# When the products with the first two tiles' gathered rows may be placed on VectorE

## The chip, the cores and the metric

The kernel runs on one core of one Trainium2 chip. The metric is the device time of one launch in microseconds (us), compared over several runs of the kernel before and after. TensorE is called PE in the profile, VectorE DVE, ScalarE ACT, GpSimd POOL and SyncE SP.

## What is computed

One block of a diffusion model over 1024 latent tokens of width 1024, with 256 context tokens beside them. First a token-mixing part: an input projection, multi-head attention (8 heads, 1280 keys, low-rank queries), a state-space branch, gates, an output projection and a layer norm. Then a channel-mixing part, PEER: each token's queries pick 128 of 16384 experts (8 heads, 16 each), and the output is a weighted sum of their rows of `v`, with a weight from the dot product of the token with their rows of `u`:

```
experts = jnp.take_along_axis(cand_e, top_pos, axis=-1)
g = jax.nn.softmax(top_s, axis=-1).astype(xb.dtype)
act = jax.nn.gelu(jnp.einsum('thkd,td->thk', u_tab[experts], xb))
return jnp.einsum('thk,thkd->td', g * act, v_tab[experts])
```

After it comes a last layer norm, and the latent stream is the output.

## The kernel before, in words

The 1024 tokens are eight tiles of 128, numbered 0 to 7. They go through the front (attention, gates, output projection, first norm) in four groups: tile 0; tiles 1 and 2; tiles 3, 4 and 5; tiles 6 and 7 (`GROUPS`). For each group `front` runs these stages one behind another:

- `attention`: for each head and tile, scores on PE (L858 to L862), maximum on DVE (L863 to L867), exponential on ACT (L872), transposes and the product with the values (L805, L809). Keys and values come from DRAM by SP's queue.
- `gates`: projections (L239 to L241) with weights that SP loads and that ACT and DVE split in two parts (L233, L234).
- `close`: the output projection (L954 to L957), two layer norms (`affine`, L181 and L182, with a chain of small steps L142 to L154 for the reciprocal root), transposes (L192). At its end `prepare` (L770 to L780) makes the compressed queries of the next group; its last VectorE step for each tile is L775, and the last of these for group g is kept as the mark `p` with that group's index (the groups are counted from 0, so that `p2` is the third group's, of tiles 3 to 5, and `p3` the fourth group's, of tiles 6 and 7).
- `route`: it picks the experts. It is a generator, whose steps run beside the next group's attention; its last step (L1103) writes the experts' numbers of tiles that are not dense.

Tiles 2 to 5 (`DENSE`) are later multiplied with all experts in a PE-bound stage, `dense` (L1196 to L1198, L1235 to L1237), which takes the rest of the span; `spread` (L1147 to L1156) makes its table of weights during the fronts. Tiles 0, 1, 6 and 7 gather only the rows that they chose. The change concerns tiles 0 and 1. For each of them `score` makes 128 gathers, one row per token and choice (L1271: POOL issues an indirect DMA of 128 rows of 4 KB, 512 KB in all), and 128 products on DVE (L1275: row times token, summed into one number). `weighted` then gathers 128 times from `v` (L1351) and sums them on PE (L1356). Gathered rows of both kinds go through six buffers in turn (`RB = 6`), and each gather waits until the one six before it has been used. `retrieve` takes tile 0's products first, then 32 of tile 0's value rows, then tile 1's products with one value row of tile 0 after every second, then the values of tile 1.

The order of instructions on each engine is fixed when the program is built, by a scheduler that takes, among instructions that its model thinks ready, the one of highest priority. The fronts have a raised priority (`PRIO`), and the retrieval of tiles 0 and 1, traced behind all four fronts, has the lowest: its products fill what is left. Each engine then works through its own queue in that fixed order on the chip.

`HOLDS` adds an edge to that. For a tile in the table, each product from a given number on may be ordered on DVE only behind a marked DVE instruction:

```
held = [m for m, n in HOLDS[l] if s >= n] if l in HOLDS else []
with tc.issue_after(marks[held[-1]].ins) if held else nullcontext():
    V.scalar_tensor_tensor(ub, ub, 1.0, h2, op0=MUL, op1=MUL, accum_out=dots[:, s:s + 1])
```

With `S0 = 36`, `P0 = 128`, `M0 = "p2"` and `S1 = 100`, `P1 = 128`, `M1 = "p3"`, tile 0's products 36 to 127 stand behind `p2`, and tile 1's products 100 to 127 behind `p3`. The further entries of the two lists begin at products 164 (36 + 128) and 228 (100 + 128) and up, which a tile of 128 products does not have.

Of the kernel before, what the change touches and what calls it, by code (L numbers as in the profile page):

```python
# [73 lines left out]
S0 = 36  # L74
P0 = 128
S1 = 100
P1 = 128
M0 = "p2"
M1 = "p3"
HOLDS = {0: [(M0, S0)] + [("r1.%d" % h, S0 + P0 * (h + 1)) for h in range(8)],  # L80
         1: [(M1, S1)] + [("r2.%d" % h, S1 + P1 * (h + 1)) for h in range(8)],
         6: [("t3", 0)]}
KENG = ((), (), (), ())
GENG = ((), (), (), ())
EVERY = (1, 2, 1)
# [4 lines left out]
def block_kernel(ctx: ExitStack, tc: tile.TileContext, a: dict, out: bass.AP):  # L90
# [1173 lines left out]
    def score(l, ei, dots):  # L1264
# [4 lines left out]
        for s in range(128):  # L1269
            ub = rows.tile([128, D], F32, tag="row", name="ub")  # L1270
            GP.indirect_dma_start(out=ub, out_offset=None, in_=a["peer_u"],  # L1271
                                  in_offset=bass.IndirectOffsetOnAxis(ap=ei[:, s:s + 1], axis=0))
            held = [m for m, n in HOLDS[l] if s >= n] if l in HOLDS else []
            with tc.issue_after(marks[held[-1]].ins) if held else nullcontext():
# [320 lines left out]
```

## Time and profile before

| | us |
|---|---|
| runs of the kernel before: median (lowest to highest of 3) | 3748.12 (3733.66 to 3753.72) |
| the profiled execution, its own time | 3734.93 |
| span of the profiled execution | 3733.2 |
| PE busy in the span | 3359.1 (90%) |
| DVE busy in the span | 2956.9 (79%) |
| POOL busy in the span | 1491.9 (40%) |

The profile cuts the span into stretches and gives for each the busy time of each engine. Beside it stand the TensorE clock that was granted, as a share of full speed, the mean busy share of the core's 16 DMA engines, and what they moved. A count behind a busy time is a number of instructions. In a timeline, a bracket at the end of a line says how long the engine was idle before the instruction and what ended that. The profiled execution runs through the stages at these times: second group's attention from 653 to 849, its gates to 918, its close with `prepare` of the third group to 980, third group's attention from 994 to 1340, its gates from 1360 to 1520, its close with `prepare` of the fourth group to 1604, fourth group's attention from 1640 on, the dense stage from 2218 to the end.

### The profile page before, as it was taken

How to read it: one execution, taken by the hardware profiler on the slowest of the kernel's cores; microseconds unless marked ns; L12 is line 12 of the kernel's file. 1: busy time of each engine (PE TensorE's matmuls, PEld its weight loads, DVE VectorE, ACT ScalarE, POOL GpSimd, SP SyncE). 2: the span in 40 equal slices, each digit the busy share in tenths (PEclk: the TensorE clock that was granted, in tenths of full speed). 3: DMA queues.
4: the chain of work that ended last, by engine and by line, in shares of the span. 5: the costliest groups of instructions: out<-in, count | busy, mean ns of one | idle time of the engine just before them, and what ended most of it. 6: DMA issues, size and time to landing. Idle time of an engine off the chain costs nothing.

```text
span 3733.2 us, 54383 instructions
## 1 busy us (share of the span) xinstructions
PE 3359.1 (90%) x20022; PEld 2733.2 (73%) x20022; DVE 2956.9 (79%) x6996; ACT 1297.7 (35%) x2329; POOL 1491.9 (40%) x1254
## 2 busy tenths in 40 slices
PE   5978888979779989869999969999999999999997
PEld 3745577869667668757769758878888888888885
DVE  7358755685798879689968877888888888889895
ACT  2223353443123444033345443333333333333332
POOL 5045400041355564443442100265655555546540
PEclk7978999989889989979999979999999999999998
DMA  8742276476698898987898763599999999989992
GB/s 280 236 85 73 89 264 228 156 301 244 224 347 309 316 338 324 362 308 289 295 355 314 296 232 124 181 368 340 330 342 333 339 335 340 340 325 355 340 328 79
DMA packets 348714, 1032.46 MB, mean 277 GB/s; under 512 B 46592, under 2 KB 142080, under 8 KB 322592
## 3 DMA queue, kind: packets, MB, share of 16 engines
q0 software_dynamic: 147456, 536.94, 39.3%
q1 hardware_dynamic: 164032, 462.20, 34.9%
q10 hardware_dynamic: 36960, 29.86, 2.5%
q8 instruction: 157, 2.57, 0.3%
q14 instruction: 109, 0.89, 0.1%
HBM read 961.27 MB, written 67.62 MB: 276 GB/s over the span
## 4 chain that ended last, share of the span: by engine, by line
PE 56%; DVE 9%; issue 8%; DMA 7%; ACT 2%; POOL 2%; DVEq 0%; POOLq 0%; ACTq 0%
PE turn L1235 6%; PE turn L1237 6%; PE turn L1236 6%; PE fd L1196 5%; PE fd L1197 5%; PE fd L1198 5%; DMA vb<-in_peer_v,eiT 4%; DVE ub L1275 3%; PE po L954 2%; PE acc L1356 2%; PE pqr L1066 2%; PE pe L1153 2%; DMA ub<-in_peer_u,ei 2%; POOL ub L1271 1%; PE po L809 1%
## 5 line engine op out<-in xcount | busy, mean ns | idle before, releaser
L1271 POOL DMA_INDIRECT ub<-in_peer_u,ei x512 | 654.9, 1279 | 1212.9 <-DVE ub L1275 438.4
L1275 DVE SCALAR_TENSOR_TENSOR ub<-ub,h 128x1024 f32<-128x1024 f32 x512 | 616.3, 1217 | 59.5 <-DMA ub<-in_peer_u,ei 59.2
L1318 POOL DMA_INDIRECT vb<-in_peer_v,ei x256 | 361.8, 1413 | 268.2 <-DVE f L1321 205.5
L1351 POOL DMA_INDIRECT vb<-in_peer_v,eiT x256 | 288.7, 1128 | 400.4 <-PE acc L1356 324.8
L1235 PE MATMUL turn<-hh,u 128*128 128x512 f32 x1024 | 401.7, 392 | 0.0
L1236 PE MATMUL turn<-hh,u 128*128 128x512 f32 x1024 | 400.2, 391 | 0.0
L1237 PE MATMUL turn<-hl,u 128*128 128x512 f32 x1024 | 400.1, 391 | 0.0
L1197 PE MATMUL fd<-v,kpe_l 128*128 128x512 f32 x887 | 351.7, 397 | 1.5 <-DVE kpe_l L234 1.5
L1198 PE MATMUL fd<-v,kpe_h 128*128 128x512 f32 x887 | 349.6, 394 | 0.0
L1196 PE MATMUL fd<-v,kpe_h 128*128 128x512 f32 x887 | 339.3, 396 | 0.0
L1321 DVE SCALAR_TENSOR_TENSOR f<-vb,zz,f 128x1024 f32<-128x1024 f32 x254 | 325.4, 1281 | 2.8 <-DMA vb<-in_peer_v,ei 0.2
L1239 ACT ACTIVATE act<-turn 128x512 f32<-128x512 f32 x128 | 76.6, 598 | 578.7 <-PE turn L1237 578.6
L233 ACT CAST v<-w 128x1024 fp32r<-128x1024 f32 x128 | 134.7, 1053 | 269.1 <-PE fd L1197 269.0
L1235 PEld LDWEIGHTS turn<-hh,u 128*128 128x128 f32 x1024 | 192.3, 188 | 42.0
L1237 PEld LDWEIGHTS turn<-hl,u 128*128 128x128 f32 x1024 | 192.3, 188 | 41.9
L1236 PEld LDWEIGHTS turn<-hh,u 128*128 128x128 f32 x1024 | 192.3, 188 | 40.4
L1356 PE MATMUL acc<-vb,diag 128*32 128x256 f32 x2048 | 159.8, 397 | 51.1 <-DMA vb<-in_peer_v,eiT 51.0
L1198 PEld LDWEIGHTS fd<-v,kpe_h 128*128 128x128 f32 x887 | 166.8, 188 | 41.4
L1196 PEld LDWEIGHTS fd<-v,kpe_h 128*128 128x128 f32 x887 | 166.9, 188 | 40.8
L1197 PEld LDWEIGHTS fd<-v,kpe_l 128*128 128x128 f32 x887 | 166.9, 188 | 40.5 <-DVE kpe_l L234 1.8
L234 DVE TENSOR_TENSOR v<-w,v 128x1024 fp32r<-128x1024 f32 x128 | 156.2, 1221 | 33.4 <-ACT v L233 32.8
L1241 DVE TENSOR_TENSOR act<-act,gt 128x512 f32<-128x512 f32 x128 | 88.6, 692 | 118.2 <-ACT act L1239 117.9
(421 smaller groups left out, 8143.2 us busy)
## 6 DMA issues: line engine op xcount, KB each, us to landing
w<-in_peer_uT SPq DMA_DIRECT2D x64, 1024.0 KB
w<-in_peer_v SPq DMA_DIRECT2D x64, 1024.0 KB
w<-in_peer_wq SPq DMA_DIRECT2D x32, 1024.0 KB
gT_d<-stage SPq DMA_DIRECT2D x16, 2048.0 KB
gt<-gT_d SPq DMA_DIRECT2D x32, 1024.0 KB
vh<-v_d SPq DMA_DIRECT2D x32, 640.0 KB
w<-k_d SPq DMA_DIRECT2D x32, 640.0 KB
w<-in_w_mod_b SPq DMA_DIRECT2D x16, 1024.0 KB
```

What stands on the lines that cost most here:

```text
L1196: PE.matmul(o, ah[:, ts], vh[:, cs], start=first, stop=False)
L1197: PE.matmul(o, al[:, ts], vh[:, cs], start=False, stop=False)
L1198: return PE.matmul(o, ah[:, ts], vl[:, cs], start=False, stop=final)
L1235: PE.matmul(turn, uh[:, k, :], hh[:, k, :], start=(k == 0), stop=False)
L1236: PE.matmul(turn, ul[:, k, :], hh[:, k, :], start=False, stop=False)
L1237: PE.matmul(turn, uh[:, k, :], hl[:, k, :], start=False, stop=(k == 7))
L1271: GP.indirect_dma_start(out=ub, out_offset=None, in_=a["peer_u"], in_offset=bass.IndirectOffsetOnAxis(ap=ei[:, s:s + 1], axis=0))
L1275: V.scalar_tensor_tensor(ub, ub, 1.0, h2, op0=MUL, op1=MUL, accum_out=dots[:, s:s + 1])
L1318: GP.indirect_dma_start(out=vb, out_offset=None, in_=a["peer_v"], in_offset=bass.IndirectOffsetOnAxis(ap=ei[:, s:s + 1], axis=0))
L1321: V.scalar_tensor_tensor(f, vb, z[:, s:s + 1], f, op0=MUL, op1=ADD)
L1351: GP.indirect_dma_start(out=vb, out_offset=None, in_=a["peer_v"], in_offset=bass.IndirectOffsetOnAxis(ap=eiT[:, t:t + 1], axis=0))
L1356: PE.matmul(acc[d // 2][o:o + 32, 256 * (d % 2):256 * (d % 2) + 256], dg[:, q, jj, :], vb[:, d * 256:(d + 1) * 256], start=False, stop=Fal ...
```

## The change

The entries of tiles 0 and 1 leave the table of holds; that of tile 6 stays. The constants that they used stay unused, and no instruction is added or removed.

```diff
@@ -77,9 +77,7 @@
 P1 = 128
 M0 = "p2"
 M1 = "p3"
-HOLDS = {0: [(M0, S0)] + [("r1.%d" % h, S0 + P0 * (h + 1)) for h in range(8)],
-         1: [(M1, S1)] + [("r2.%d" % h, S1 + P1 * (h + 1)) for h in range(8)],
-         6: [("t3", 0)]}
+HOLDS = {6: [("t3", 0)]}
 KENG = ((), (), (), ())
 GENG = ((), (), (), ())
 EVERY = (1, 2, 1)
```

## Rows read from the trace of the kernel before

**Rows 1.** The page: the group of products (busy, mean ns, idle before).

```profile
L1275 DVE SCALAR_TENSOR_TENSOR ub<-ub,h 128x1024 f32<-128x1024 f32 x512 | 616.3, 1217 | 59.5 <-DMA ub<-in_peer_u,ei 59.2
```

**Rows 2.** Busy time by stretch: all engines, granted clock, DMA share, GB/s.

```profile
653.00:773.00 120.00, 112.24 (x800) 102.10 (x798) 85.20 (x375) 53.52 (x158) 4.89 (x6) 1.00 0.45 150
773.00:850.00 77.00, 56.02 (x337) 49.19 (x335) 64.95 (x130) 35.57 (x79) 47.94 (x35) 0.84 0.93 351
861.00:918.00 57.00, 54.46 (x455) 54.26 (x454) 30.58 (x39) 21.27 (x22) 0.00 (x0) 1.00 0.60 214
918.00:948.00 30.00, 30.00 (x138) 26.17 (x137) 14.95 (x40) 0.60 (x1) 0.00 (x0) 0.94 0.65 217
948.00:980.00 32.00, 23.19 (x169) 21.70 (x168) 21.52 (x87) 4.46 (x14) 0.00 (x0) 0.85 0.30 109
994.00:1160.00 166.00, 130.15 (x879) 114.14 (x877) 158.96 (x498) 51.24 (x133) 95.00 (x84) 0.90 0.94 346
1160.00:1232.00 72.00, 67.12 (x568) 48.72 (x569) 61.46 (x320) 21.03 (x57) 25.88 (x27) 0.95 0.74 262
1360.00:1520.00 160.00, 146.40 (x1228) 134.89 (x1228) 128.59 (x266) 59.75 (x67) 74.20 (x56) 0.96 0.90 337
1520.00:1581.00 61.00, 53.69 (x283) 41.47 (x284) 44.21 (x110) 1.79 (x3) 32.39 (x27) 0.94 0.93 350
1581.00:1604.00 23.00, 16.75 (x139) 13.93 (x137) 22.30 (x90) 3.38 (x7) 3.62 (x4) 0.87 0.74 288
1604.00:1640.00 36.00, 17.59 (x80) 9.76 (x81) 26.66 (x45) 9.31 (x19) 24.81 (x21) 0.56 0.90 318
1640.00:2217.00 577.00, 518.27 (x4148) 419.64 (x4148) 474.30 (x1706) 251.13 (x424) 181.33 (x174) 0.95 0.82 303
2217.00:3733.00 1516.00, 1484.38 (x6696) 1210.56 (x6695) 1287.57 (x2058) 494.74 (x690) 714.21 (x512) 0.99 0.83 298
```

The columns of this view are: stretch, length, PE, PE weight loads, DVE, ACT, POOL, then clock, DMA share and GB/s.

**Rows 3.** The same view for L1275 alone (two instructions a product, busy on DVE).

```profile
773.00:850.00 77.00, 40.78 (x68) 0.84 0.93 351
994.00:1160.00 166.00, 102.04 (x168) 0.90 0.94 346
1360.00:1520.00 160.00, 44.05 (x73) 0.96 0.90 337
1520.00:1581.00 61.00, 21.47 (x36) 0.94 0.93 350
```

**Rows 4.** Timeline of POOL, where the first hold ends.

```profile
981.64 1.68 POOL L1271 DMA_INDIRECT ub<-in_peer_u,ei  x1 [124.44 <-DVE ub L1275]
```

**Rows 5.** Timeline of DVE around the two marks (the accumulator reads are each product's second instruction).

```profile
979.61 0.62 DVE L775 TENSOR_SCALAR nq<-pa,rs_y 128x384 f32<-128x384 f32 x1
980.15 1.22 DVE L1275 SCALAR_TENSOR_TENSOR ub<-ub,h 128x1024 f32<-128x1024 f32 x1
...
1578.88 1.21 DVE L1275 SCALAR_TENSOR_TENSOR ub<-ub,h 128x1024 f32<-128x1024 f32 x1
...
1603.25 0.61 DVE L775 TENSOR_SCALAR nq<-pa,rs_y 128x384 f32<-128x384 f32 x1
1603.78 1.22 DVE L1275 SCALAR_TENSOR_TENSOR ub<-ub,h 128x1024 f32<-128x1024 f32 x1
...
1609.59 0.14 DVE L153 TENSOR_SCALAR rs_t<-rs_t 128x1 f32<-128x1 f32 x1
```

**Rows 6.** Timeline of PE behind the second mark.

```profile
1612.59 1.08 PE L1356 MATMUL acc<-vb,diag 128*32 128x256 f32 x8 [8.76 <-DMA vb<-in_peer_v,eiT]
1619.42 1.08 PE L1356 MATMUL acc<-vb,diag 128*32 128x256 f32 x8 [5.75 <-DMA vb<-in_peer_v,eiT]
...
1624.86 0.90 PE L778 MATMUL ptc<-eye,nq 128*128 128x128 f32 x3
```

**Rows 7.** Timeline of DVE: tile 1's experts are known.

```profile
1232.22 0.22 DVE L1103 CAST ei<-ef 128x128 int32<-128x128 f32 x1
```

**Rows 8.** Timeline of PE: the first product of the dense stage.

```profile
2217.65 0.48 PE L1235 MATMUL turn<-hh,u 128*128 128x512 f32 x1
```

## The prediction

> **What bounds the kernel now.** I read the table by stretch first, then the same table for the products alone, then the timelines at the two marks. The dense stage fills 2217 to 3733 with PE busy for 1484 of 1516 us [rows 2], and its first product runs at 2217.65 [rows 8]. Nothing of the change lies in it, so the change is worth what it moves this start. Before that the four fronts run one behind another, and the time of each stage is set by PE's work and by what delays PE. As a yardstick I take PE's busy time times the granted clock as its work, and the rest of a stretch as lost. The last attention stretch before any product, 653 to 773, loses 120 - 112.24 x 1.00 = 7.8 us, 6.5%. With products it is another stage: 773 to 850 loses 77 - 56.02 x 0.84 = 29.9 us, and 994 to 1160 loses 166 - 130.15 x 0.90 = 48.9 us, with DVE busy for 158.96 of 166 [rows 2]. The granted clock shows part of it: 1.00 before the first product, 0.84 and 0.90 beside them.
>
> The first hold is easy to see. POOL's gather at 981.64 had idled for 124.44 us behind a product that waited [rows 4], and that product runs at 980.15, right behind `p2` at 979.61 [rows 5]. Meanwhile DVE was busy for 30.58 of 57, 14.95 of 30 and 21.52 of 32 us [rows 2], so 52 us of it lay idle in the gates, the output projection and `prepare`. The second hold lasts from the product at 1578.88 to the one at 1603.78 [rows 5], but there DVE was full: 22.30 of 23 us [rows 2].
>
> **The change, part by part.** Nothing is added or removed. 92 products of tile 0 (36 to 127) and 28 of tile 1 (100 to 127) may move ahead of the marks, each with its gather on POOL's queue and 512 KB on the DMA engines. A product costs DVE 1.217 us [rows 1], with its accumulator read 102.04 / 84 = 1.21 us of busy time in the dense pattern of 994 to 1160 [rows 3]. The entries that begin at product 164 and 228 never bound anything; dropping them costs nothing.
>
> How many of tile 0 move: the front's instructions keep their priority, so the products take what is left, at the pace of the later stages of the same kind, which ran with rows in flight. The gates of the third group took 56 gathers in 160 us, one in 2.86; its output projection 27 in 61, one in 2.26 [rows 2]. At these paces 861 to 918 takes 20, 918 to 948 13, and 948 to 980 at the second pace 14: 47 products. 45 are left at 980.
>
> What they cost where they go: the gates of the third group lost 160 - 146.40 x 0.96 = 19.5 us, those of the second, without products, 57 - 54.46 = 2.5, or 4.5%. On 160 us that is 7.1, and the other 12.3 go to some 36 products [rows 2, 3] and the value rows and `spread` beside them: at most 0.34 us a product. The output projection lost 61 - 53.69 x 0.94 = 10.5 against 30 - 30.00 x 0.94 = 1.8 (6%): 6.9 over 18 products, 0.38 each. So 20 x 0.34 + 13 x 0.38 = 12 us. In `prepare` the path is a chain of small DVE steps with 10.5 us idle between them; 14 products need 17 us, so 6 or 7 push: 8 us. Sum 20. Bounds: nothing, if all fits into the 52 us of idle DVE time (47 products need 57, so nearly); above, the price of 773 to 850, (29.9 - 5.0) / 34 = 0.73 each for the first 33, and the full 17 in `prepare`: 41.
>
> What they give back where they leave: 994 to 1160 lost 48.9, of which 6.5% or 10.8 would be lost without products; 38.1 over 84 is 0.45 a product, times 47 is 21 us. Bounds: nothing (PE was busy for 130 of 166, and another limit may take DVE's place), and 47 x 0.73 = 34. The first hold nets -1 us, between +41 and -34: I expect the gain and the price nearly to cancel.
>
> What is late next: tile 0's products end near 1065 instead of 1159, its 32 value rows follow, and then POOL stands still until tile 1's experts are known. That is set by `route`, at 1232.22 [rows 7]; the stretch before it, 1160 to 1232, has no products already and loses only 72 - 67.12 x 0.95 = 8 us [rows 2]. So the earlier end of tile 0's products is worth nothing by itself; what counts is whether the front and `route` come earlier.
>
> The second hold: in 25 us, at one row in 2.26 us and two products to one value row, 7 products move ahead of `p3`. DVE is full there, so up to 7 x 1.21 = 8.5 us land on `prepare`; with part of them between steps that wait for PE or ACT I take 5, at least nothing. Against that stands what the release does now: five held products run in a row from 1603.78 to 1609.59 ahead of a step of the norm [rows 5], and PE, in its fixed order, stands 8.76 and 5.75 us before value rows that POOL could only fetch late, with the transposes of the new queries behind them at 1624.86 [rows 6]. 1604 to 1640 loses 36 - 17.59 x 0.56 = 26.1 us, against 37% (8.4 of 23) in the stretch ahead of it [rows 2]; at 37% it would lose 13.2. I take 12 of these 13 back, between 0 and 13. Net -7, between +8.5 and -13.
>
> From there to 2217 the work stays as it is, and a shift of the front passes through: PE is busy for 518 of these 577 us [rows 2].
>
> Sum: +20 - 21 + 5 - 12 = -8 us. The profiled execution took 3734.93 us, which would become 3727; it lies 13 us under the median of the runs, 3748.12, and against the median the forecast is 3740. A measurement of this kernel can tell about 0.5% from no change, 19 us; the forecast is inside that.
>
> **The rivals.** A, slower: the gathers and the products get in the way of the gates. SP's weights and POOL's gathers share the DMA engines. In 773 to 850 these were 0.93 busy at 351 GB/s; 861 to 918 needs 214 GB/s without a gather, so 137 are free, room for one gather in 3.8 us and not in 2.86 [rows 2]. DVE takes products in a fixed order, and one whose row is late holds the splits of the weights behind it, and with them PE. Price: the upper bounds, 41 us before 980 and 8.5 before 1604, less the 21 given back later and nothing regained behind `p3`: +28, 3776. It decides from the point at which a moved product costs 0.4 us (19 / 47) more where it goes than where it was. For it speaks 773 to 850, at 0.73 a product; against it, that the third group's gates ran at 0.90 DMA and PE still 146 of 160 us busy.
> The Trainium skill, DMA: Bandwidth & Descriptors, section Queues, rings and completion order, says that a DMA engine takes turns between the queues that have work for it, packet by packet. By that rule alone two busy queues halve the 351 GB/s, the weights would come at 175 instead of 214, and the second group's gates would take 57 x 214 / 175 = 70 us, 13 more instead of 7; the sum would be -2. The third group's gates, at 337 GB/s with both queues in use, do not show PE starved in this way, so I keep 7.
>
> B, faster: DVE is what holds attention back, and all of the price per product of 773 to 850 comes off: 34 us there, 13 behind `p3`, for 12 us in the gates and projection and nothing in the two `prepare`: -35, 3713. For it: DVE 158.96 of 166 and the idle 52 us before. Against it: the same stretch holds `route` of two tiles, which needs DVE as well.
>
> C, the change does next to nothing: the scheduler has no idle slot for the products before the marks and orders them as now. Against it: 52 idle us. It would give 3748.
>
> **How the numbers follow.** The forecast with its neighbours within 19 us, C among them, gets 0.40; A 0.30; B 0.30: the two signs rest on terms of equal size (20 against 21) with equal bounds. Faster by over 0.5% 0.30, within 0.5% 0.40, slower 0.30. The range reaches from beyond B, 3702, to beyond A, 3782; the bounds taken all together (+50 and -47) lie at 3798 and 3701, and I leave out what is above 3782. The forecast's own range is 3729 to 3767.
>
> **What the profile after would show.** If right: no wait of POOL over 100 us near 860; products 36 to 127 spread over 856 to about 1065; DVE over 45 of 57 us in the second group's gates; the third group's first score some 20 us later than 994, its attention after that shorter by as much; PE's two stops behind `p3` gone; the dense stage's first product within some 19 us of 2217. Wrong in A's way: PE under 90% in the second group's gates, with ACT and DVE waiting for weights, and a first score of the third group 30 us or more later. Wrong in B's way: DVE well under 90% in the third group's attention and tile 1's experts known before 1210. What I cannot bound from the rows is the new order itself: every instruction of the fronts is placed afresh around the products, and a different order of a few critical steps may weigh as much as my terms.

## The result: slower by 0.8%, and not by the stage that was feared

| | before | changed |
|---|---|---|
| median of 5 runs, us (lowest to highest) | 3741.06 (3733.66 to 3753.72) | 3774.97 (3765.84 to 3775.98) |
| ratio to before (95% interval) | | 1.0083 (1.0062 to 1.0104) |
| span of the profiled execution, us | 3733.2 | 3774.1 |
| the dense stage's first product at, us | 2217.65 [rows 8] | 2251.95 |

The change costs about 31 us (23 to 39). The forecast was 8 us less, a change too small to be measured: 3740 against a median of 3748. The range held the time, and rival A gave 3776.

Source lines behind the edit are two lower in the changed kernel: the products are L1273, the last step of `prepare` for a tile is L773. The table by stretch of the changed kernel, in the columns of [rows 2], first the second group's gates, projection and `prepare`, then the third group's attention, then the fourth group's `prepare` and what follows:

```profile
866.00:927.00 61.00, 56.54 (x469) 56.14 (x468) 54.23 (x79) 22.10 (x24) 28.46 (x20) 0.99 0.98 378
927.00:961.00 34.00, 31.74 (x139) 27.06 (x137) 24.65 (x50) 0.60 (x1) 17.93 (x15) 0.92 0.95 348
961.00:1034.00 73.00, 24.31 (x167) 22.23 (x166) 66.00 (x178) 4.57 (x14) 46.60 (x37) 0.65 0.89 329
1047.00:1170.00 123.00, 114.72 (x916) 92.73 (x915) 84.21 (x370) 40.45 (x109) 39.18 (x39) 0.97 0.72 260
1170.00:1250.00 80.00, 75.65 (x543) 67.66 (x542) 60.24 (x307) 29.78 (x80) 0.00 (x0) 0.98 0.25 87
1601.00:1634.00 33.00, 18.22 (x153) 14.02 (x151) 31.23 (x108) 4.32 (x8) 17.27 (x14) 0.76 0.93 346
1634.00:1660.00 26.00, 16.98 (x80) 9.64 (x81) 21.57 (x41) 7.47 (x16) 19.38 (x16) 0.58 0.96 356
1660.00:2252.00 592.00, 526.99 (x4148) 429.43 (x4146) 472.08 (x1702) 252.32 (x426) 188.19 (x171) 0.93 0.79 293
2252.00:3774.00 1522.00, 1486.11 (x6690) 1210.47 (x6689) 1290.64 (x2058) 492.30 (x691) 715.08 (x512) 0.99 0.83 297
```

Set beside [rows 2]: the gates took 61 us instead of 57, with DVE at 54.23 instead of 30.58; the projection 34 instead of 30; and `prepare` 73 instead of 32, with PE busy for 24.31 us against 23.19 and the granted clock at 0.65 instead of 0.85. Of the two levels, 1.2 and 2.4 GHz, PE mostly had the lower one there, after its long stops. The third group's attention shows what was given back: its first 123 us ran at 0.97 of the clock and PE 114.72 us busy, and the first score that came 53 us late (1047 against 994) had become 18 us by the time tile 1's experts were known (1249.92 against 1232.22 [rows 7]). PE's own queue says where the time in `prepare` went. This is its timeline there, with the idle time ahead of an instruction and what ended it in brackets:

```profile
988.07 5.49 PE L768 MATMUL pa<-wcq,hm 128*128 128x128 f32 x24 [15.85 <-DVE rs_t L151]
...
1018.12 1.09 PE L190 MATMUL tp<-eye,xr 128*128 128x128 f32 x4 [20.80 <-DVE xr L180]
...
1034.44 0.87 PE L776 MATMUL ptc<-eye,nq 128*128 128x128 f32 x3 [9.60 <-DVE nq L773]
```

Three stops, 46 us in all, each ended by DVE. In the kernel before, the two longest stops there were these:

```profile
964.05 8.49 PE L770 MATMUL pa<-wcq,hm 128*128 128x128 f32 x48 [3.26 <-DVE rs_v L142]
...
980.38 0.87 PE L778 MATMUL ptc<-eye,nq 128*128 128x128 f32 x3 [3.10 <-DVE nq L775]
```

And this is DVE in the changed kernel, ahead of the second of its stops:

```profile
1001.18 0.15 DVE L140 TENSOR_SCALAR rs_v<-bn_a 128x1 f32<-128x1 f32 x1
1001.25 1.27 DVE L179 SCALAR_TENSOR_TENSOR xr<-xr,bn_a,tab 128x1024 f32<-128x1024 f32 x1
1002.44 1.22 DVE L1273 SCALAR_TENSOR_TENSOR ub<-ub,h 128x1024 f32<-128x1024 f32 x1
1003.58 0.08 DVE L1273 DVE_READ_ACCUMULATOR ub<-ub,h 128x1 f32 x1
1003.58 0.15 DVE L143 TENSOR_SCALAR rs_y<-rs_v 128x1 int32<-128x1 int32 x1
1003.65 1.21 DVE L1273 SCALAR_TENSOR_TENSOR ub<-ub,h 128x1024 f32<-128x1024 f32 x1
1004.79 0.08 DVE L1273 DVE_READ_ACCUMULATOR ub<-ub,h 128x1 f32 x1
1004.79 1.22 DVE L1273 SCALAR_TENSOR_TENSOR ub<-ub,h 128x1024 f32<-128x1024 f32 x1
1005.93 0.08 DVE L1273 DVE_READ_ACCUMULATOR ub<-ub,h 128x1 f32 x1
1005.93 0.15 DVE L144 TENSOR_SCALAR rs_y<-rs_y 128x1 int32<-128x1 int32 x1
1006.00 1.23 DVE L1273 SCALAR_TENSOR_TENSOR ub<-ub,h 128x1024 f32<-128x1024 f32 x1
1007.16 0.08 DVE L1273 DVE_READ_ACCUMULATOR ub<-ub,h 128x1 f32 x1
1007.16 0.24 DVE L147 SCALAR_TENSOR_TENSOR rs_t<-rs_y,rs_v 128x1 f32<-128x1 f32 x1
```

The reciprocal root of a norm is a chain of steps, each of 0.15 to 0.25 us and each in need of the one before. One or two products of 1.2 us stand in every gap: L143, L144 and L147 start 1.2 to 2.4 us apart. With the hold such a chain runs undisturbed. From a second profile of the kernel before, taken beside the experiments, the chain of the last tile's queries up to the mark:

```profile
967.25 0.15 DVE L142 TENSOR_SCALAR rs_v<-ss 128x1 f32<-128x1 f32 x1 [2.02 <-ACT nq L773]
967.44 0.15 DVE L145 TENSOR_SCALAR rs_y<-rs_v 128x1 int32<-128x1 int32 x1
967.63 0.15 DVE L146 TENSOR_SCALAR rs_y<-rs_y 128x1 int32<-128x1 int32 x1
967.81 0.22 DVE L149 SCALAR_TENSOR_TENSOR rs_t<-rs_y,rs_v 128x1 f32<-128x1 f32 x1
...
969.80 0.62 DVE L775 TENSOR_SCALAR nq<-pa,rs_y 128x384 f32<-128x384 f32 x1
```

Twelve steps in 2.6 us, one in some 0.2 us. The same chain in the changed kernel took 8.3 us, with three products in it; ahead of two of them DVE stood idle until their rows landed, and the chain stood behind them:

```profile
1025.36 0.15 DVE L140 TENSOR_SCALAR rs_v<-ss 128x1 f32<-128x1 f32 x1
1027.13 1.23 DVE L1273 SCALAR_TENSOR_TENSOR ub<-ub,h 128x1024 f32<-128x1024 f32 x1 [1.62 <-DMA ub<-in_peer_u,ei]
...
1029.76 1.23 DVE L1273 SCALAR_TENSOR_TENSOR ub<-ub,h 128x1024 f32<-128x1024 f32 x1 [0.89 <-DMA ub<-in_peer_u,ei]
...
1033.67 0.62 DVE L773 TENSOR_SCALAR nq<-pa,rs_y 128x384 f32<-128x384 f32 x1
```

### The profile page after: what moved, and what is told of

It is laid out like the page before. It is cut to its first block, busy times and chain, and to the rows that moved or that the text cites. A ratio compares the mean times of both kernels' runs of the same rounds, so it can differ in the third digit from the quotient of the medians.

```text
span 3774.1 us, 54370 instructions
## 1 busy us (share of the span) xinstructions
PE 3383.1 (90%) x20022; PEld 2751.5 (73%) x20022; DVE 2963.7 (79%) x6996; ACT 1293.0 (34%) x2329; POOL 1512.0 (40%) x1254
## 4 chain that ended last, share of the span: by engine, by line
PE 60%; DVE 10%; DMA 8%; issue 4%; ACT 2%; POOL 1%; DVEq 0%; POOLq 0%; ACTq 0%
PE turn L1233 6%; PE turn L1234 6%; PE turn L1235 6%; PE fd L1194 5%; PE fd L1195 5%; PE fd L1196 5%; DMA ub<-in_peer_u,ei 4%; DMA vb<-in_peer_v,eiT 3%; PE pqr L1064 3%; PE po L952 2%; PE acc L1354 2%; DVE ub L1273 2%; PE pe L1151 2%; PE po L807 2%; PE pg L237 1%
## 5 line engine op out<-in xcount | busy, mean ns | idle before, releaser
L1269 POOL DMA_INDIRECT ub<-in_peer_u,ei x512 | 674.2, 1317 | 1219.8 <-DVE ub L1273 357.6
L1273 DVE SCALAR_TENSOR_TENSOR ub<-ub,h 128x1024 f32<-128x1024 f32 x512 | 616.0, 1218 | 61.6 <-DMA ub<-in_peer_u,ei 54.3
```

## The experiments

The runs before and after lay in several sets; the kernel before had medians of 3741 to 3759 us in them. Each run is therefore read by its ratio to the runs of before in its own set. Where an expectation names a time, it was written against 3741.

**One hold at a time.** The first two kernels put back one hold each; the third begins tile 0's hold later; the fourth lets tile 0's products from 36 on go only behind the output projection, so that gates and projection are clear of them and `prepare` is not.

```diff
keep_first
+HOLDS = {0: [(M0, S0)], 6: [("t3", 0)]}
keep_second
+HOLDS = {1: [(M1, S1)], 6: [("t3", 0)]}
first_68
+HOLDS = {0: [(M0, 68)], 1: [(M1, S1)], 6: [("t3", 0)]}
prep_only
+HOLDS = {0: [("w1", S0)], 1: [(M1, S1)], 6: [("t3", 0)]}
-                V.scalar_tensor_tensor(x[:, cs], x[:, cs], ALPHA, t, op0=MUL, op1=ADD)
+                marks["w%d" % gi] = V.scalar_tensor_tensor(x[:, cs], x[:, cs], ALPHA, t, op0=MUL, op1=ADD)
```

> Only tile 0's hold is back (products 36 to 127 behind p2); tile 1's stays away. Theory 1 (the whole price is tile 0's products between the small steps of the third group's prepare): the time of the kernel before, 3741 within 10 us, third group's first score near 994 and prepare of the third group about 31 us long. Rival (both holds share the loss, the second one some 10 to 15 us of it): 3755.

Measured: 1.0062 (1.0036 to 1.0088).

> Only tile 1's hold is back (products 100 to 127 behind p3); tile 0's stays away. Theory 1: as the changed kernel, 3775 within 10 us, third group's first score near 1047. Rival (both holds share the loss): 3760.

Measured: 1.0031 (1.0013 to 1.0049). Both miss theory 1. The two losses add up, within the intervals, to that of the change: 0.62% with tile 1 free and 0.31% with tile 0 free, against 0.83%. So tile 1's 28 products carry more of it than tile 0's 92.

> Both holds are there, but tile 0's begins at product 68 instead of 36: 32 more products are free in the second group's gates and output projection, and prepare stays clear of them. Theory 1 (prepare's chain has the price, gates and projection are cheap, at most 0.4 us a product): third group's first score 994 to 1008, attention after it shorter by 10 to 15 us, time 3725 to 3745. Rival A as predicted (the price lies in gates and projection, by the weights' loads): 3760 or more.

Measured: 0.9992 (0.9975 to 1.0008), first score at 1000.6. Rival A's 3760 did not come, and the gain in the attention did not either: gates and projection took 6 to 7 us more, and the third group's attention 347.1 us, as before, with 30 products fewer in it.

> Tile 0's products 36 to 127 stand behind the last step of the second group's output projection instead of p2, so that the gates and the projection are clear of them and prepare is not; tile 1's hold is back. Theory 1: prepare is 60 us or longer, third group's first score 1025 to 1040, time 3760 to 3780. Rival A as predicted: first score within 10 us of 994, time that of the kernel before, 3741.

Measured: 1.0106 (1.0080 to 1.0132), by the median more than the change itself (the intervals overlap), with the gates and the projection untouched and the first score at 1048.8, later than theory 1's 1025 to 1040. The rival is out.

The stages of these kernels in us, from their timelines (the gates end with the first product of the output projection, `prepare` runs from its last product to the mark, attention from the first score to the last product with the values), and the number of products that start in them:

| second to third group | before | before, again | changed | keep_second | first_68 | prep_only |
|---|---|---|---|---|---|---|
| gates | 69.3 | 70.8 | 73.4 | 72.9 | 73.4 | 69.3 |
| projection | 30.0 | 29.9 | 33.3 | 32.6 | 33.4 | 29.9 |
| `prepare` | 31.4 | 28.6 | 73.0 | 69.0 | 29.7 | 89.5 |
| products in `prepare` | 0 | 0 | 36 | 35 | 0 | 54 |
| attention | 346.0 | 349.1 | 313.0 | 309.9 | 347.1 | 320.0 |
| products in attention | 124 | 124 | 51 | 51 | 94 | 72 |

From a mean of 30 us without products, `prepare` grows by 43 us with 36, 39 with 35 and 59.5 with 54: 1.1 to 1.2 us a product, nearly its whole 1.21 us on DVE. Gates and projection pay 3 us each for 25 and 14 products, 0.1 to 0.25. Attention gives back 34.5 us for 73 products, 0.47 each, against the mean of the two profiles of before; by the spread told at the end it may be 33 to 45. For the change: 3 + 3 + 43 - 34.5 = 15 us; for keep_second 3 + 3 + 39 - 37.6 = 7, where its ratio gives 12 (5 to 18).

**DVE or the DMA engines?** In `prepare` of the changed kernel the DMA engines were 0.89 busy, where before they had 0.30. To part the two, the products keep their gathers and work on a sixteenth of the columns; tile 1 is held.

```diff
short_products
+HOLDS = {1: [(M1, S1)], 6: [("t3", 0)]}
-                V.scalar_tensor_tensor(ub, ub, 1.0, h2, op0=MUL, op1=MUL, accum_out=dots[:, s:s + 1])
+                V.scalar_tensor_tensor(ub[:, 0:64 if l == 0 and s >= S0 else D], ub[:, 0:64 if l == 0 and s >= S0 else D], 1.0, h2[:, 0:64 if l == 0 and s >= S0 else D], op0=MUL, op1=MUL, accum_out=dots[:, s:s + 1])
```

> Tile 0 is free as in the changed kernel (tile 1 is held), with all its gathers, but its products 36 to 127 work on 64 of the 1024 columns (so these dot products are left incomplete). Theory 1 (a product's 1.2 us of DVE between each two of prepare's small steps is the price): prepare of the third group back at 30 to 42 us, first score of that group by 1010. Rival (the gathers' DMA traffic is the price): prepare stays at 60 us or more.

Measured, in one execution: `prepare` took 35.5 us and the first score came at 1000.5. Its stretch in the table by stretch:

```profile
951.30:986.80 35.50, 23.88 (x168) 22.02 (x166) 22.17 (x110) 4.58 (x14) 15.40 (x16) 0.78 0.96 361
```

The same stretch for the products alone (busy time on DVE, two instructions a product, then clock, DMA share and GB/s):

```profile
951.30:986.80 35.50, 3.00 (x30) 0.78 0.96 361
```

With the DMA engines 0.96 busy, fuller than in the changed kernel, and 15 products of 0.2 us, `prepare` is nearly back. The same row of the products alone for keep_second, then for prep_only:

```profile
951.23:1020.27 69.04, 43.23 (x72) 0.64 0.94 345
```

```profile
946.00:1035.60 89.60, 65.14 (x108) 0.62 0.93 338
```

43 us of products made it 39 longer, 65 made it 60 longer. So it is the products' time on DVE, and the traffic is at most 4 to 7 us of it, by the 28.6 and 31.4 us that `prepare` took in the kernel before. What the traffic costs shows in DVE's waits in `prepare` (total us, times, longest). First the kernel before, then the changed one:

```profile
DVE h2T L112 <- PE tp L192: 6.2, 1, 6.2
DVE xr L181 <- DMA h_d<-xr: 3.1, 1, 3.1
DVE rs_v L142 <- ACT nq L773: 2.0, 1, 2.0
```

```profile
DVE ub L1273 <- DMA ub<-in_peer_u,ei: 6.2, 6, 2.1
```

The three waits of before, 9.5 us of them inside [rows 2]'s stretch with its 10.5 us of idle time, are gone: products did fill them. In their place DVE, which works in a fixed order, stood for products whose rows had not landed.

**What the second hold is worth.** Without it, 9 products run in the fourth group's `prepare`, but 7 fewer behind it, up to the first score, and the next first score came no later by this (22.2 + 36.1 us before, 32.2 + 27.8 in keep_first). Its loss appears further on. Two values of the hold between the two kernels tell the number of products from the order of the rest: the orders of PE and SP that the scheduler makes behind `p3` are, at 106, exactly those without the hold, and at 108 others. Up to the fourth group's `prepare` all of them have one order with the kernel before, which was profiled once more beside them.

```diff
s1_106, s1_108
+HOLDS = {0: [(M0, S0)], 1: [(M1, 106)], 6: [("t3", 0)]}
+HOLDS = {0: [(M0, S0)], 1: [(M1, 108)], 6: [("t3", 0)]}
```

> The kernel before itself, to have its stages on the same chip as the others and to see what two sets of its own runs differ by: ratio 1.000 within 0.003; third group's attention 346 to 358 us, fourth group's attention 285 to 295 us, prepare of the third group about 30 us.

Measured: 0.9992 (0.9978 to 1.0006).

> Tile 1's hold begins at product 106 instead of 100 (tile 0's as before): six more products may run ahead of p3. The orders of PE and SP behind that are exactly those of the kernel without tile 1's hold, while at 108 they are others. Theory P (each product in the fourth group's prepare costs time): between the kernel before and the one without tile 1's hold, ratio 1.003 to 1.006, and 108 at least as slow. Theory O (it is the order of the fourth group's attention that the free products lead to): 1.006 as without the hold, with 108 somewhere else.

Measured: 1.0063 (1.0041 to 1.0085).

> Tile 1's hold begins at product 108: as many products run ahead of p3 as with 106 or two more, but the orders of PE and SP in the fourth group's attention are another set. Theory P: ratio 1.004 to 1.007. Theory O: not bound to the value of 106, and likely back at 1.000 to 1.002.

Measured: 1.0040 (1.0025 to 1.0056). This does not decide between the theories. At 106 the loss is that of keep_first (1.0062) with 5 products in `prepare` instead of 9, and the traces show the same order of PE, SP, ACT and POOL in the two kernels; that is what theory O expected. Against theory P, 108 was not slower than 106, though two more products ran in `prepare`; against theory O, the other order of 108 loses too. The intervals of the two overlap.

| fourth group, us | before | before, again | changed | keep_first | s1_106 | s1_108 |
|---|---|---|---|---|---|---|
| `prepare` | 22.1 | 22.2 | 32.5 | 32.2 | 29.8 | 31.0 |
| products in it | 0 | 0 | 9 | 9 | 5 | 7 |
| to the first score | 36.2 | 36.1 | 26.2 | 27.8 | 32.1 | 31.9 |
| attention | 284.7 | 297.2 | 294.9 | 306.1 | 307.5 | 300.6 |
| from there to the dense stage | 293.5 | 296.6 | 297.6 | 301.2 | 300.7 | 303.5 |

"Before" and "changed" are of one set, the rest of later sets, keep_first of another set than its neighbours. Against the "before" of its own set, or the one profiled again, each kernel without the hold loses 15 to 18 us from the end of the projection to the dense stage: 0 to 5 up to the first score, 3 to 10 in the attention, 4 to 7 behind it. One such profile shows no loss by itself: prep_only, which has the second hold, took 664 us there, and before and before again, with one order, 636 and 652. The ratios show it. The stretches of keep_first show `prepare`, and the attention with no more work on PE than in the second profile of before, which is in the fence behind it:

```profile
1598.70:1630.90 32.20, 18.44 (x154) 14.21 (x152) 30.82 (x107) 4.23 (x8) 14.89 (x13) 0.77 0.87 331
1630.90:1658.70 27.80, 15.89 (x78) 8.72 (x79) 21.26 (x40) 7.02 (x14) 20.77 (x17) 0.59 0.96 351
1658.70:1964.80 306.10, 279.55 (x2208) 214.32 (x2207) 228.97 (x1053) 112.18 (x272) 127.54 (x125) 0.97 0.82 290
```

```profile
1580.50:1602.70 22.20, 16.11 (x137) 13.70 (x137) 21.23 (x85) 3.38 (x7) 2.58 (x3) 0.88 0.75 291
1602.70:1638.80 36.10, 17.48 (x81) 9.34 (x79) 26.76 (x47) 8.87 (x18) 25.32 (x20) 0.56 0.88 306
1638.80:1936.00 297.20, 278.05 (x2154) 212.69 (x2151) 232.39 (x1061) 110.98 (x270) 122.44 (x121) 0.97 0.82 293
```

Part of the 9 us in the attention goes with PE's wait for value rows. The waits of PE in the attention, first keep_first, then before again (total us, times, longest):

```profile
PE acc L1356 <- DMA vb<-in_peer_v,eiT: 16.9, 9, 4.7
```

```profile
PE acc L1356 <- DMA vb<-in_peer_v,eiT: 9.6, 5, 3.0
```

To see whether the products' time on DVE is behind it or the rows and the order, tile 1's products 100 to 127 were cut to 64 columns, with and without the hold:

```diff
short_held, short_free
-                V.scalar_tensor_tensor(ub, ub, 1.0, h2, op0=MUL, op1=MUL, accum_out=dots[:, s:s + 1])
+                V.scalar_tensor_tensor(ub[:, 0:64 if l == 1 and s >= S1 else D], ub[:, 0:64 if l == 1 and s >= S1 else D], 1.0, h2[:, 0:64 if l == 1 and s >= S1 else D], op0=MUL, op1=MUL, accum_out=dots[:, s:s + 1])
short_held
+HOLDS = {0: [(M0, S0)], 1: [(M1, S1)], 6: [("t3", 0)]}
short_free
+HOLDS = {0: [(M0, S0)], 6: [("t3", 0)]}
```

> Both holds as before, but tile 1's products 100 to 127 work on 64 of the 1024 columns (so these dot products are left incomplete): 28 products of 1.2 us less on DVE behind p3. It is the base for the next run. Time up to 20 us under the kernel before, 0.994 to 1.000; prepare of the fourth group 22 us.

Measured: 0.9982 (0.9968 to 0.9996).

> As the run before this one (tile 1's products 100 to 127 on 64 columns, left incomplete), with tile 1's hold away. Theory P (the DVE time of the products that run ahead of p3 is the price of the second hold): the loss of 0.4 to 0.6% goes, within 0.2% of the run with the hold, prepare of the fourth group 22 to 25 us. Rival G (it is the rows and the order: gathers and value rows that run earlier, and what they meet in the fourth group's attention): still 0.4 to 0.6% slower than with the hold.

Measured: 0.9978 (0.9964 to 0.9992). With short products the hold is worth nothing, as theory P expected. But the rows and the order were not held equal: behind `p3` PE's order in short_free is another than in keep_first, and by the end of the fourth group's attention PE had used some 197 value rows, as in the kernel before (some 199), where keep_first had used some 208 (s1_108, which loses too, some 200). So it is not shown whether the second loss hangs on the products' length on DVE or on the order that comes with it.

**Other places for the holds.** Two last kernels try whether a longer hold does better: tile 1's from product 88, tile 0's from product 12.

```diff
s1_88, s0_12
+HOLDS = {0: [(M0, S0)], 1: [(M1, 88)], 6: [("t3", 0)]}
+HOLDS = {0: [(M0, 12)], 1: [(M1, S1)], 6: [("t3", 0)]}
```

> Both holds are there, tile 1's begins at product 88 instead of 100: the output projection of tiles 3 to 5 gets clear of 12 products as well, and 12 more are left for the fourth group's attention. If each product on the way to the queries costs what it costs DVE, projection gets 3 to 6 us shorter and the attention behind it longer by as much or less: 0.997 to 1.001, possibly a kernel that beats the one before. If the later order decides, anything to 1.006.

Measured: 1.0014 (0.9997 to 1.0031). The projection was 1 to 2 us shorter and the fourth group's attention 14 us longer than in the second profile of before.

> Both holds are there, tile 0's begins at product 12 instead of 36: 24 products leave the second group's attention, where a product cost about 0.73 us, for the third group's, where it is worth about 0.55. If these prices add up: 24 x 0.73 = 17 us less before, 24 x 0.55 = 13 us more behind, 0.997 to 1.001. Rival: tile 0's products end some 35 us later, its 32 value rows are not through when tile 1's experts are known, tile 1's products start later than that by 20 us or more and the value rows are late for the dense stage: 1.003 to 1.008.

Measured: 1.0020 (1.0006 to 1.0033), between the two ranges. The second group's attention behind its experts became 63.2 us long instead of 74.5, but everything of tile 1 moved back, and 9 of its products, all under number 100, fell into the fourth group's `prepare`, which took 33.3 us as in the changed kernel:

```profile
1576.80:1610.10 33.30, 19.23 (x162) 14.24 (x160) 29.60 (x104) 3.28 (x7) 16.25 (x14) 0.77 0.88 330
```

With the same 9 products in that stretch keep_first has 1.0062, so the length of the fourth group's `prepare` alone does not make the second loss. Among the kernels with whole products none was found that beats the one before.

## Why the prediction was wrong

**The step that failed** for the first hold is the price in `prepare`: "948 to 980 at the second pace 14", of which "6 or 7 push: 8 us", at most 17. Measured: 36 products and 43 us. Both halves were off, the count more than the rest: with 36 products the same working gives 36 x 1.21 - 10.5 = 33 us. The count took the stretch's length as given; at the same pace, one in 2.26 us, the 73 us that it became hold 32 products. How many stand ahead of the mark is fixed by the scheduler, and why it put 36 there was not looked into. The other 10 us are the idle time of DVE, which was counted as room, 10.5 of 32 us [rows 2]. 9.5 us of it lay in three waits, for PE, ACT and a DMA, each long enough for a product. The products did take their place, but DVE then stood idle for 6.2 us ahead of products whose rows had not landed, with the chain behind them, so that little was won. The same holds for "52 us of it lay idle" as cover: it was cover in the gates and the projection only.

**The terms that held.** The gates and the projection were priced at 12 us and cost 6 to 7. The gain in the third group's attention was put at 0.45 a product and came out at 0.47; as 73 products left instead of 47, it was 34.5 us instead of 21. That the price per product fits is no proof of it, as 30 products fewer were worth nothing in first_68. With the measured count and price in `prepare` the first hold nets +15, not -1; keep_second's ratio gives 12.

**The second hold** was put at -7 us, for 12 us taken back at the burst behind `p3`. By keep_first's ratio it is +23 us (14 to 33), the larger of the two misses. The stretch to the first score shrank from 36 to 26 us as forecast, though PE's two stops before value rows became shorter and did not go. In the changed kernel they are:

```profile
1634.45 1.08 PE L1354 MATMUL acc<-vb,diag 128*32 128x256 f32 x8 [3.52 <-DMA vb<-in_peer_v,eiT]
1640.76 1.08 PE L1354 MATMUL acc<-vb,diag 128*32 128x256 f32 x8 [5.23 <-DMA vb<-in_peer_v,eiT]
```

The price in `prepare` was 10 us instead of 5, and these two cancel. The step that failed here is "From there to 2217 the work stays as it is, and a shift of the front passes through", which puts everything behind the first score at nothing. From there to the dense stage keep_first, s1_106 and s1_108 took 607, 608 and 604 us, and the kernel before, in the set of the last two, 594 (578 in its first profile). The cause of this loss stays open. The longer wait for value rows, 16.9 against 9.6 us, is a part; whether the products' length on DVE or the order that comes with them makes the rest was not shown.

**A shift of the front passes through**: for the first hold right, as far as can be told. Its shift is what is left of 53 us when tile 1's experts are known, 18, and 20 at the last product of the third group's attention (1360.3 against 1340.5).

**Rival A** gave 3776 and the measured time is 3775, but by another road. It put the price into the gates, by weights that come late. The gates ran with the DMA engines at 0.98 and 378 GB/s and were 3 to 4 us longer. Its bound for `prepare`, 17 us, was too low as well, and the agreement of the sums is chance. Of its signs, PE under 90% in the gates did not come (56.54 of 61); the first score 30 us late or more did, by 53 us, but through `prepare`. What it said of DVE, that a product whose row is late holds what stands behind it, is seen in `prepare`, for 6.2 us.
The Trainium skill (DMA: Bandwidth & Descriptors, Queues, rings and completion order) says that a DMA engine takes turns between the queues that have work for it. The trace of the changed kernel's gates agrees. Its two queues there, the gathers and then SP's loads (packets, MB, share of the 16 engines' time):

```profile
q0 software_dynamic: 3189, 11.58, 49.2%
q1 hardware_dynamic: 1702, 11.42, 48.0%
```

What failed is the working in the prediction that made the gates 13 us longer by this rule: it halved 351 GB/s, and the two queues had 378. With 378 the same working gives, as an estimate, 57 x 214 / 189 = 65 us, 8 more, and 3 to 4 were measured.

**Rival B** expected nothing in the two `prepare` and is out by that. Its gain of 34 us in the attention came (34.5), closer than the spread of that stage lets one tell.

## What to carry to other kernels

Work of low priority that fills an engine's queue was cheap here, 0.1 to 0.25 us for a product of 1.2 us, in stretches that PE's work bounds, and dear in a chain of short dependent steps on the same engine: there each filler cost nearly its whole length. Idle time in the sum of the stretch was no cover, since fillers that stand in a fixed order bring waits of their own. So look, before a hold is taken away or put in, at the single steps and waits and not at the busy share; and count the fillers for the lengthened stretch. And a hold can be worth more behind its mark than at it, as the second one here, so each hold should be taken away alone.

## What the runs showed that was not expected

The same order of instructions takes different times from one execution to the next, stage by stage: the third group's attention, in the same order in all of them, took 346.0, 349.1, 357.8, 347.3 and 353.4 us in before, before again, keep_first, s1_106 and s1_108. A difference of 10 us in one stage of one profile is therefore no finding here; the ratios carry the verdicts, and the stage tables are read only where several kernels agree or the difference is 30 us and more.

Thirty products fewer in the third group's attention (first_68) were worth nothing that this spread lets one see, where 73 fewer were worth 34.5 us: the gain does not look to be in proportion.
